# The gate's sigmoid from ScalarE's exponential and VectorE's reciprocal, with a replanned order of instructions

## The chip, the cores and the metric

The kernel runs on one core of one Trainium2 chip. The metric is the device time of one execution in microseconds (us); for the kernel before it is the median of three runs.

The engines are called by the profile's names: PE is TensorE's matrix products and PEld its weight loads, ACT is ScalarE, DVE is VectorE, POOL is GpSimd, and SP is SyncE, which issues the transfers.

## What is computed

One inference step of a two-layer decoder trunk for a prompt of 512 tokens and 64 sample tokens (8 sequences of 8), which share all weights, at model width 1024. Layer 0 mixes tokens by pooling, layer 1 by a gated DeltaNet; a SwiGLU feed-forward network of inner width 2816 follows each, and every block has a norm before and after it.

The change lies in the DeltaNet layer's gates. Cut to that, the reference is:

```python
b = proj[..., ...]; a = proj[..., ...]        # 16 value heads each
beta = jax.nn.sigmoid(b.astype(jnp.float32))
g = -jnp.exp(a_log) * jax.nn.softplus(a + dt_bias)
o, s_new = gated_delta_chunked(q, k, v, g, beta, s0)
```

`gated_delta_chunked` uses beta as a factor on keys and values, and sums of g, through exponentials, as decays.

## The kernel before

**Tiling and stages.** Activations stand with 128 channels on the partitions and 576 tokens along the free axis, split into two halves of 256 and 320 (for the feed-forward blocks 288 and 288). Each large matrix product is made of three products of split operands (`hH`, `hL` for the activations, `wh`, `wl` for the weights): ACT rounds the raw weight tile `wraw` into `wh`, DVE or POOL subtracts to give `wl`, and PE multiplies. The stages are, in order: the pooling mixer, a first feed-forward block, the DeltaNet layer in four groups of heads (loop `for G in range(GRP)`), its output projection, and a second feed-forward block.

**The start.** `tokens(tt)` (line 1235) takes a block of 128 tokens `xt`, sums its squares on ACT, takes a square root `xst`, and on DVE a reciprocal (line 1244) and the scaled tokens `xn`. The first products, against the pooling matrices `bf`, `bm` and `bh`, read `xn`. The masks `bs`, `s_in`, `s_le`, `s_st` and others are also made in that time, on POOL and DVE, for later stages.

**The gates.** `gates()` (line 1387) is called inside the first group's projection. The small tiles it uses are pieces of one buffer, `misc`. It multiplies the activations with 32 columns of the weight matrix, brings the result to token order in `ab`, takes `bet` as ACT's sigmoid of half of it, and from the other half `g`, by a softplus written as an exponential and a logarithm on ACT with DVE instructions between. The products of `g` with the triangular masks give running sums: one is copied to `gcr` by ACT and sent to the DRAM tile `gc_d`, from which decay tiles are read later. The tile `gcr` has the tag `T01`, and so does `gts` (line 1646), which the first group's sample part writes next: the later tile waits until the earlier one has been read. `bet` is scaled by the key norms later on, when the chain `rv`, `rn` on DVE has the inverse norms, and `Uw`, `BD`, `vn` read it.

**The order of the work.** All instructions from line 803 on are not issued as they are written. They are collected by the class `Plan`, with operands and dependences, and `finish` (line 431) issues them in an order that it works out when the program is built. `cost` (line 312) holds a duration for each kind of instruction. `forward` (line 568) plays the program through with one queue for each engine and picks, whenever an engine comes free, the ready instruction of best rank. `backward` turns the times of an order into due times, which are the next ranks. Where an instruction may run on DVE or POOL (`EITHER`), `forward` chooses. The transfers on SP are ordered in the same way.

ACT holds one table of functions at a time. `TABLE` (line 72) numbers the functions that need one (SiLU, exponential, square root, sigmoid, logarithm), and `TURN` gives a change of table 1283 ns in the plan. `take` (line 748) picks the next instruction of an engine; where `HOLD` is above zero for that engine, it passes over the best one if that needs another table (on PE, another mode of the array) and one that needs none is ready within `HOLD` ns of it in rank.

`forward` also keeps a picture of PE's clock: work is added up in windows of `WINDOW` ns, in four phases, since the place of the windows is not known, and a phase with less work than `LOAD` of the window has its next one at half clock. In gaps of PE over 300 ns, `idle_until` (line 614) puts in matmuls of a tile of ones into an unused bank; they are the ones written to `ps_w` from line 474.

At last, `refined` (line 480) goes over the whole order once for each string of `CHOSEN` (line 80): at each point in time it moves the ranks of coming instructions by amounts that `moved` (line 499) derives from the numbers listed there. These numbers were found by a search beforehand and stand in the source as data.

Because every planned instruction is issued from one place, nearly all lines of the profile show the same line number, 478; instructions are told apart by the tiles that they write and read.

Of the kernel before, what the change touches and what calls it, by code (L numbers as in the profile page):

```python
# [14 lines left out]
AF = mybir.ActivationFunctionType  # L15
# [27 lines left out]
VH = 16  # L43
# [14 lines left out]
class Plan:  # L58
# [15 lines left out]
    HOLD = {"PE": 2500.0, "ACT": 0.0}  # L74
    WINDOW, LOAD = 3413.0, 0.38
# [492 lines left out]
    def forward(self, rank, state=None, until=None):  # L568
# [4 lines left out]
        if state is None:  # L573
            todo = n
            left = [len(o[4]) for o in ops]
            free = dict.fromkeys(self.ENGINES, 0.0)
# [5 lines left out]
            phases = [[self.WINDOW * i / 4, 0.0, 2.0, 0, self.WINDOW * (4 - i) / 4] for i in range(4)]  # L582
            fast = 2.0
# [1601 lines left out]
```

## Time and profile before

| what | value |
|---|---|
| median of three runs | 1514.92 us (1513.43 to 1515.28) |
| the profiled execution | 1514.92 us |
| its span, from the first to the last instruction | 1513.2 us |
| mean granted clock of PE | 0.995 |
| PE busy | 1492.4 us, 99% of the span, 11790 matmuls |
| DVE busy | 1130.1 us, 75% |
| ACT busy | 852.2 us, 56% |
| POOL busy | 112.1 us, 7% |
| data moved by DMA | 197.86 MB, mean 131 GB/s |

In rows of the busy time by stage, the first figure after the stretch is its length, then comes each engine's busy time with its number of instructions, the granted clock of PE, the share of the DMA engines that was busy, and GB/s. In rows of the timeline, the first figure is the start in us from the span's start, the second the duration; a bracket at the end gives the idle time of the engine before it and what ended it. In rows of groups, behind the count stand the busy time in us, the mean of one in ns, and the idle time before. Rows of waits give the total in us, the number, and the longest. Matmuls overlap, so the interval from start to start, not the duration of one, is what a matmul takes of PE.

### The profile page before, as it was taken

Reading aid. Unit: us, or ns where it says so; the run is one execution under the profiler, and the core shown is the slowest. Engines: PE = TensorE matmul, PEld = TensorE weight load, DVE = VectorE, ACT = ScalarE, POOL = GpSimd, SP = SyncE. Lnnn points to the kernel's source line nnn. Section 1 sums busy time; section 2 is a strip of 40 time slices with the busy share of each in tenths; the row PEclk is TensorE's granted clock in tenths of the full one; section 3 lists DMA queues with packets and bytes.
Section 4 is the critical chain, followed back from the end, with each engine's and each line's share of the span. In section 5 each row is a group of like instructions: output and inputs, shape, how many; then the busy total and the mean of one; then the engine's idle time right before and its main releaser. Section 6 shows DMA issues by size and latency. Waiting matters only on the chain.

```text
span 1513.2 us, 30277 instructions
## 1 busy us (share of the span) xinstructions
PE 1492.4 (99%) x11790; PEld 1445.6 (96%) x11790; DVE 1130.1 (75%) x2280; ACT 852.2 (56%) x1839; POOL 112.1 (7%) x246
## 2 busy tenths in 40 slices
PE   8999999999999999999999999999999999999998
PEld 7999999999999899899899899899999999999997
DVE  6994566668789697996898798657796575756856
ACT  7763543435456865865684794645575453434545
POOL 4210000000001010110121110000110000000000
PEclk9999999999999999999999999999999999999999
DMA  7564233233467343434443534657864432324264
GB/s 191 146 184 127 83 88 92 80 102 111 125 181 194 90 126 111 125 99 125 130 113 94 147 113 127 199 157 215 248 193 145 127 97 86 93 81 121 65 163 136
DMA packets 344854, 197.86 MB, mean 131 GB/s; under 512 B 13499, under 2 KB 337692, under 8 KB 344703
## 3 DMA queue, kind: packets, MB, share of 16 engines
q1 hardware_dynamic: 344711, 195.92, 44.9%
q8 instruction: 93, 1.52, 0.4%
q14 instruction: 50, 0.41, 0.1%
HBM read 165.60 MB, written 30.52 MB: 130 GB/s over the span
## 4 chain that ended last, share of the span: by engine, by line
PE 57%; DVE 4%; ACT 2%; DMA 2%; issue 1%; SPq 0%; ACTq 0%; DVEq 0%
PE ps_m L478 16%; PE ps_A L478 15%; PE ps_B L478 14%; PE ps_s L478 5%; PE ps_k L478 4%; PE ps_x L478 2%; DVE vt L478 1%; DVE ac L478 1%; PE ps_n L478 1%; DMA vt<-z_d 1%; DVE wl L478 1%; DVE ii L478 0%; DMA out_dram<-St 0%; ACT wh L478 0%; DMA og<-og_d 0%
## 5 line engine op out<-in xcount | busy, mean ns | idle before, releaser
L478 ACT ACTIVATE wh<-wraw 128x1024 fp32r<-128x1024 f32 (+4 forms) x239 | 233.3, 979 | 202.6 <-PE ps_B L478 87.2
L478 DVE TENSOR_TENSOR wl<-wraw,wh 128x1024 fp32r<-128x1024 f32 (+4 forms) x238 | 266.2, 1123 | 82.8 <-ACT wh L478 48.1
L478 PE MATMUL ps_m<-hH,wh 128*128 128x320 f32 (+1 forms) x832 | 246.9, 311 | 0.3 <-ACT zz L478 0.3
L478 PE MATMUL ps_m<-hL,wh 128*128 128x320 f32 (+1 forms) x832 | 245.6, 307 | 0.0
L478 PE MATMUL ps_m<-hH,wl 128*128 128x320 f32 (+1 forms) x832 | 244.7, 307 | 0.0
L478 PEld LDWEIGHTS ps_m<-hH,wh 128*128 128x128 f32 x832 | 153.7, 189 | 4.3 <-issue 1.5
L478 PEld LDWEIGHTS ps_m<-hH,wl 128*128 128x128 f32 x832 | 154.1, 189 | 2.6 <-issue 1.3
L478 PEld LDWEIGHTS ps_m<-hL,wh 128*128 128x128 f32 x832 | 154.4, 189 | 1.9 <-issue 0.6
L478 PE MATMUL ps_B<-hH,wl 128*128 128x320 f32 (+1 forms) x444 | 128.7, 304 | 0.0
L478 PE MATMUL ps_B<-hL,wh 128*128 128x320 f32 (+1 forms) x444 | 128.4, 303 | 0.0
L478 PE MATMUL ps_B<-hH,wh 128*128 128x320 f32 (+1 forms) x444 | 128.0, 304 | 0.0
L478 PE MATMUL ps_A<-hH,wl 128*128 128x256 f32 (+1 forms) x432 | 118.9, 291 | 0.0
L478 PE MATMUL ps_A<-hH,wh 128*128 128x256 f32 (+1 forms) x432 | 118.8, 290 | 0.0
L478 PE MATMUL ps_A<-hL,wh 128*128 128x256 f32 (+1 forms) x432 | 118.4, 289 | 0.0
L478 PE MATMUL ps_A<-aL,wh 128*128 128x288 f32 (+2 forms) x408 | 113.8, 296 | 0.0
L478 PE MATMUL ps_A<-aH,wl 128*128 128x288 f32 (+2 forms) x408 | 113.4, 296 | 0.0
L478 PE MATMUL ps_A<-aH,wh 128*128 128x288 f32 (+2 forms) x408 | 113.2, 296 | 0.0
L478 PE MATMUL ps_B<-aH,wl 128*128 128x288 f32 x296 | 83.7, 297 | 0.1
L478 PE MATMUL ps_B<-aH,wh 128*128 128x288 f32 x296 | 83.0, 296 | 0.1
L478 PE MATMUL ps_B<-aL,wh 128*128 128x288 f32 x296 | 83.1, 295 | 0.0
L478 PEld LDWEIGHTS ps_B<-hH,wh 128*128 128x128 f32 x444 | 81.8, 188 | 0.3
L478 PEld LDWEIGHTS ps_B<-hH,wl 128*128 128x128 f32 x444 | 81.8, 188 | 0.1
(458 smaller groups left out, 3976.9 us busy)
## 6 DMA issues: line engine op xcount, KB each, us to landing
wraw<-in_ffn_w_in_dram SPq DMA_DIRECT2D x77, 512.0 KB
wraw<-in_gdn_w_in_dram SPq DMA_DIRECT2D x56, 512.0 KB
graw<-in_ffn_w_in_dram SPq DMA_DIRECT2D x33, 512.0 KB
wraw<-in_ffn_w_out_dram SPq DMA_DIRECT2D x32, 448.0 KB
wraw<-in_gdn_w_out_dram SPq DMA_DIRECT2D x24, 512.0 KB
wraw<-in_ffn_w_out_dram SPq DMA_DIRECT2D x32, 320.0 KB
St<-in_state_gdn_rec_dram SPq DMA_DIRECT2D x32, 256.0 KB
out_dram<-St SPq DMA_DIRECT2D x32, 256.0 KB
```

The costliest lines, as they stand in the source:

```text
L478: calls[e](*a, **k)
```

## The change

The sigmoid of the gates becomes an exponential of the negated input on ACT, an addition of 1 and a reciprocal on DVE, all in place in `bet`.

The planner is changed with it. `HOLD` for ACT goes from 0 to 1500 ns. `LOAD` goes from 0.38 to 0.40. The engines start at the times of `BEGIN`, not at zero. PE's clock is taken as full at the start (factor 1.0, before 2.0), and the first decision on it falls at `FIRST` plus a window or more. The data of `CHOSEN` are replaced: 5 strings with 2871 numbers, where there were 4 with 2377. Costs, dependences and everything else that is computed stay as they are.

```diff
     TABLE = {"Silu": 1, "Exp": 2, "Sqrt": 3, "Sigmoid": 4, "Ln": 5}
     TURN = {"PE": (130.0, 190.0), "ACT": (1283.0, 1283.0)}
-    HOLD = {"PE": 2500.0, "ACT": 0.0}
-    WINDOW, LOAD = 3413.0, 0.38
+    HOLD = {"PE": 2500.0, "ACT": 1500.0}
+    WINDOW, LOAD = 3413.0, 0.40
+    BEGIN = {"PE": 0.0, "ACT": 2250.0, "DVE": 2250.0, "POOL": 2200.0, "SP": 150.0}
+    FIRST = 4250.0
     SPARE = 1.5
...
     CHOSEN = (
-        "0: 7936 55843 86527 33991 97722 31117 8629 9687 47150 83676 16297 15132 53952 77128 31040 66847 59628 "
...
+        "0: 73658 29519 30370 59469 65203 80151 85529 43101 5733 57126 23353 4237 50459 50735 10507 95687 49324 "
...
@@ -573,14 +605,14 @@
-            free = dict.fromkeys(self.ENGINES, 0.0)
+            free = dict(self.BEGIN)
...
-            phases = [[self.WINDOW * i / 4, 0.0, 2.0, 0, self.WINDOW * (4 - i) / 4] for i in range(4)]
-            fast = 2.0
+            phases = [[0.0, 0.0, 1.0, 0, self.FIRST + self.WINDOW * (1.0 + i / 4)] for i in range(4)]
+            fast = 1.0
...
@@ -1423,7 +1455,9 @@
             ab = piece(SP1, 2 * VH)
             ACT.activation(ab, ps, AF.Copy)
-            ACT.activation(bet, ab[:, :, :VH], AF.Sigmoid)
+            ACT.activation(bet, ab[:, :, :VH], AF.Exp, scale=-1.0)
+            DVE.tensor_scalar(bet, bet, 1.0, None, op0=add)
+            DVE.reciprocal(bet, bet)
             ea = piece(VH)
             ACT.activation(ea, row[:, 0], AF.Exp)
```

322 rows, old and new, of the table CHOSEN are left out of this document.

## The prediction

> **What bounds the kernel now.** I read the head of the page first, then the busy time by stage, then who waits for whom, and last the timelines of the two places that the diff touches most plainly: the first 18 us and the gates of the DeltaNet layer.
>
> ```profile
> span 1513.2 us, 30277 instructions
> PE 1492.4 (99%) x11790; PEld 1445.6 (96%) x11790; DVE 1130.1 (75%) x2280; ACT 852.2 (56%) x1839; POOL 112.1 (7%) x246
> ...
> core 0: us, PE busy (x) PEld busy (x) DVE busy (x) ACT busy (x) POOL busy (x), PEclk, DMA share, GB/s
> 0.00:50.00 50.00, 45.25 (x300) 41.39 (x300) 34.95 (x99) 38.10 (x95) 19.80 (x79) 0.93 0.57 156
> 50.00:400.00 350.00, 349.98 (x2626) 348.47 (x2626) 247.45 (x401) 166.54 (x261) 10.47 (x10) 1.00 0.38 110
> 400.00:1050.00 650.00, 641.39 (x5441) 603.00 (x5440) 526.35 (x1251) 420.77 (x1118) 68.04 (x143) 1.00 0.49 139
> 1050.00:1500.00 450.00, 450.00 (x3396) 448.92 (x3395) 315.03 (x519) 222.23 (x357) 13.83 (x14) 1.00 0.45 132
> 1500.00:1513.20 13.20, 5.73 (x35) 3.81 (x34) 6.33 (x12) 4.52 (x12) 0.00 (x0) 0.72 0.47 151
> ```
>
> TensorE is the bound. Between 50 and 400 us and between 1050 and 1500 us it idles 0.02 us in 800 us at full clock; no order of the same matmuls wins anything there. What a new order can move lies in three places: the start (50.00 - 45.25 = 4.75 us idle, and the only granted clock below 1 ahead of the end), the DeltaNet stage (650.00 - 641.39 = 8.6 us idle) and the tail (13.20 - 5.73 = 7.5 us). Nothing in the diff touches the tail's own chain. ScalarE and VectorE have room on the whole (56% and 75%); they matter where TensorE waits for them:
>
> ```profile
> engine line waited for: us in total, times, longest us
> PE ps_x L478 <- DVE vt L478: 3.4, 5, 1.5
> PE ps_A L478 <- DVE xn L478: 2.3, 1, 2.3
> ...
> PE ps_s L478 <- DVE rv L478: 1.2, 1, 1.2
> PE ps_x L478 <- DMA crow<-in_state_gdn_conv_dram: 1.2, 1, 1.2
> PE ps_x L478 <- ACT nco L478: 1.0, 2, 0.7
> ```
>
> Two of these waits, the 2.3 us on xn and the 1.2 us laid to rv, are single events that the diff reaches.
>
> **Part 1, the planner's picture of the start.** The old planner starts all engines at 0 and holds the matrix clock to be slow (factor 2.0). The new one starts ScalarE, VectorE and GpSimd 2.2 us late and holds the clock to be full. What the chip did:
>
> ```profile
> 1.27 2.93 PE L474 MATMUL ps_w<-ones 128*128 128x128 f32 x12 [1.27 <-POOL ones L253]
> ...
> 6.04 0.28 ACT L478 ACTIVATE xst<-xst,epsd 128x1 f32<-128x1 f32 x1
> ...
> 8.47 0.38 DVE L478 COPY s_le<-s_le 64x64 f32<-64x64 f32 x1
> 8.57 0.28 DVE L478 RECIPROCAL xst<-xst 128x1 f32<-128x1 f32 x1
> 8.91 0.75 DVE L478 TENSOR_SCALAR xn<-xt,xst 128x1024 f32<-128x1024 f32 x1
> ...
> 9.71 0.49 PE L478 MATMUL ps_A<-bf,xn 128*128 128x128 f32 x2 [2.27 <-DVE xn L478]
> ```
>
> The square root that the first token block needs is done at 6.32 (6.04 + 0.28). Its reciprocal starts only at 8.57, behind mask work in VectorE's in-order queue: 2.25 us, nearly the whole 2.27 us for which TensorE then stands. A planner that lets VectorE begin at 0 expects those masks to be long over by then. One that begins it at 2.25 us sees the reciprocal ready ahead of them and will put it first. The masks (bs, s_in, s_le) have no early reader on TensorE, so they can follow at no cost. I price this at up to 2.2 us of the first idle.
>
> Right behind that gap the clock falls:
>
> ```profile
> 10.65:17.48 6.83, 6.54 (x30) 6.24 (x30) 4.72 (x12) 4.78 (x10) 3.53 (x10) 0.50 1.01 285
> 18.00:30.00 12.00, 11.45 (x97) 10.80 (x97) 7.22 (x17) 12.00 (x32) 2.36 (x1) 1.00 0.73 168
> 40.00:60.00 20.00, 20.00 (x150) 18.77 (x149) 19.73 (x57) 15.43 (x40) 6.36 (x8) 1.00 0.54 157
> ...
> 13.15 0.78 PE L474 MATMUL ps_w<-ones 128*128 128x128 f32 x2
> ...
> 16.82 0.41 PE L478 MATMUL ps_A<-dH,wl 128*128 128x256 f32 x1
> 17.03 0.41 PE L478 MATMUL ps_A<-dH,wh 128*128 128x256 f32 x1
> ...
> 21.06 0.28 PE L478 MATMUL ps_A<-dH,wh 128*128 128x256 f32 x1
> 21.18 0.28 PE L478 MATMUL ps_A<-dL,wh 128*128 128x256 f32 x1
> ```
>
> In the 6.83 us at 0.50 the 256-column matmuls follow each other every 0.21 us (16.82 to 17.03), afterwards every 0.12 (21.06 to 21.18). At full clock that stretch's work would take half, so 3.4 us are at stake if the gap ahead of it closes, or is filled with idle matmuls, and the clock holds. The bounds for the start are therefore 0 and 2.2 + 3.4 = 5.6 us. Against the whole of it speaks that ScalarE is full from 18 to 30 us (12.00 of 12.00) and VectorE from 40 to 60 (19.73 of 20.00): what TensorE gains ahead of them passes on only as far as their own work also starts earlier. It does in part, since ScalarE is busy only 4.78 of 6.83 us in the slow stretch. Neither end has the better row, so I take half, **2.8 us**.
>
> On the clock a page speaks against the new constants: the Trainium skill, TensorE: Matmul & The Clock Gate, Part 1, says that the throttled state is the default and activity releases it, so that a kernel's first matmuls run at half rate. The trace disagrees: the first twelve matmuls, at 1.27 us, take 2.93 us together, 0.24 each, where two of the same kind at 13.15, in the stretch at 0.50, take 0.39 each.
>
> **Part 2, the sigmoid.** It removes one activation with its table load and adds one exponential and two VectorE instructions.
>
> ```profile
> 523.15 0.83 PE L478 MATMUL ps_g<-t_le,misc 128*16 128x128 f32 x6
> ...
> 523.30 1.28 ACT L478 ACT_TABLE_LOAD   x1
> 524.59 0.27 ACT L478 ACTIVATE bet<-misc 128x80 f32<-128x80 f32 x1
> 524.77 0.57 ACT L478 ACTIVATE gcr<-ps_g 16x512 f32<-16x512 f32 x1
> ...
> 525.37 3.55 DMA gc_d<-gcr
> ...
> 528.94 0.42 DVE L478 TENSOR_TENSOR gts<-s_in,gHL 128x256 fp32r<-128x256 f32 x1 [1.30 <-DMA gc_d<-gcr]
> ...
> 500.00:530.00 30.00, 28.78 (x242) 24.96 (x241) 21.51 (x54) 28.07 (x79) 0.55 (x5) 1.00 0.23 65
> ```
>
> The load (1.28 us) and the sigmoid stand in ScalarE's queue ahead of the copy gcr, whose PSUM input is complete at 523.98 (523.15 + 0.83); gcr starts at 524.77. Its transfer to gc_d ends at 528.92, and only then may gts be written, because it shares gcr's buffer (tag T01); TensorE's "1.2 us on rv" is really this DMA. With the sigmoid gone from that spot, gcr can start 524.77 - 523.98 = 0.8 us earlier and the wait shrinks by the same. What is then late next is VectorE's norm chain for rv, so I take **0.8 us** and not the whole 1.2. The exponential for bet can stand beside the softplus's exponential on the same table; it needs its own load only if the order puts it elsewhere, and then this part gains 0 to 0.8 us.
>
> The additions:
>
> ```profile
> L478 DVE RECIPROCAL oss<-oss 128x20 f32<-128x20 f32 x4 | 1.1, 272 | 1.0 <-ACT oss L478 1.0
> L478 DVE RECIPROCAL nrc<-nrc 128x3 f32<-128x3 f32 x4 | 0.7, 170 | 0.4 <-ACT nrc L478 0.3
> L478 DVE SCALAR_TENSOR_TENSOR misc<-misc 128x80 f32<-128x80 f32 x3 | 0.7, 242 | 3.5 <-ACT misc L478 3.4
> ...
> L478 DVE TENSOR_TENSOR bet<-bet,rn x8: 161/164/170, 531.4 to 884.7; 128x10 f32<-128x10 f32 x8
> ...
> L478 ACT ACT_TABLE_LOAD x25 | 32.1, 1283 | 2.4 <-DMA misc<-in_gdn_a_log_dram 2.0
> ```
>
> The add of 80 elements costs about 0.24 us (the 128x80 row). No reciprocal of 80 is in the trace; from 3 to 20 elements it grows by 102 ns, 6 ns an element, which puts 80 at 272 + 60 x 6 = 0.63 us, an estimate. Together 0.87 us on VectorE, hidden: it is busy 21.51 of 30 us there and stands 3.4 us waiting for ScalarE's misc just before. Bet's first reader comes at 531.4 us. Without that cover it would cost its 0.87 us.
>
> **Part 3, ScalarE stays with its table.** HOLD for ScalarE rises from 0 to 1500: an activation that needs another table is passed over while one on the current table is less than 1.5 us behind it in rank. 25 loads take 32.1 us. Fewer loads free ScalarE, but TensorE waits for ScalarE by name hardly at all (nco, 1.0 us). At best that 1.0 us goes; at worst a passed-over activation is late for a matmul, which is a rival below. I take **0.4 us**.
>
> **Part 4, a new order everywhere.** The list of drawn seeds is replaced, five passes for four. Every engine's order changes in the DeltaNet stage; the other long stages are full whatever the order. Its bounds are its idle time, 8.6 us: all of it could go, or as much again could come. The new passes search against a start that resembles the trace, with one pass more, so I lean to a gain, but by a tenth only: **0.9 us**.
>
> **Sum.** 2.8 + 0.8 + 0.4 + 0.9 = 4.9 us off. The profiled execution took 1514.92 us (span 1513.2 and 1.7 around it), which is also the median of the three runs. 1514.9 - 4.9 = **1510.0 us**.
>
> **The rivals.**
>
> *The start's gain is absorbed* (chance 0.16). ScalarE, then VectorE, both full behind the start, keep their pace and the middle draws even: 1514.9 - 0.8 = 1514.1, within 1512 to 1517. For it: the 12.00 of 12.00. Against it: their work feeds on TensorE's and would move with it.
>
> *The held table makes TensorE wait* (0.20), the case on the slower side. A passed-over exponential or SiLU stands up to 1.5 us longer, and the transposes and products that read it wait; the profile's own waits of that kind are 0.7 us long at most (nco). If a dozen switches cost TensorE 0.7 us each, that is 8.4 us against 2.8 + 0.8 gained: 1514.9 + 8.4 - 3.6 = 1519.7. It decides from about six such waits up (4.2 us). For it: VectorE (526 of 650 us) and ScalarE (421) are fuller in that stage than in the other two long ones. Against it: the old order meets nearly all its table switches without TensorE noticing, and the limit is in rank, so urgent work still comes first.
>
> *The clock falls again* (0.06). Believing the clock full at the start, the planner puts fewer idle matmuls there; one more 6.83 us stretch at 0.50 costs 3.4 us, and with gcr's 0.8 us the time is 1517.5. The page on the clock gate would have it so; the twelve quick first matmuls speak against it.
>
> *Everything comes at its upper end* (0.10). 5.6 + 0.8 + half of the 8.6: 1504.2.
>
> That the change does not do what it says (bet's exponential with a load of its own) costs at most Part 2's 0.8 us and stays inside the forecast.
>
> **How the numbers follow.** Two tenths of a per cent, 3 us, is about what a measurement of this kernel can tell from no change; the three runs span 1.9 us. My forecast has chance 0.48, with a range of its own of 1506 to 1511.9. Faster: 0.48 + 0.10 = 0.58; same: 0.16; slower: 0.20 + 0.06 = 0.26. The range runs from 1503.0, a little below the upper-end case, to 1519.5, which leaves out half of the held-table case and the far edge of the other.
>
> **What would show it.** Right: the reciprocal of xst directly after its square root, the 2.27 us ahead of the first bf matmul below 1 us, a shorter stretch at 0.50; in the gates one load fewer and gcr straight after its matmuls, gts no longer held 1.3 us by gc_d; fewer than 25 table loads; 400 to 1050 us with 6 to 10 us of idle. Wrong: over 12 us idle in that stage with ScalarE named as releaser, or a start as long as before although its gap is closed.

## The result, and the profile after

| kernel | median | runs |
|---|---|---|
| before, on the same chip | 1514.28 us | 9 runs, 1512.40 to 1515.95 |
| after | 1516.81 us | 9 runs, 1516.27 to 1520.19 |

The ratio is 1.0026, with a 95% interval of 1.0018 to 1.0034. The change makes the kernel slower, by 0.26% over all its runs and by 2.5 us in the medians (its other runs lie further above the median than below it); the forecast was 1510.0, faster. The profiled execution took 1516.81 us. Its page, and the busy time by stage (us of the stretch, then PE, PEld, DVE, ACT, POOL, the granted clock, DMA share, GB/s):

```profile
span 1514.9 us, 30387 instructions
PE 1496.5 (99%) x11836; PEld 1448.4 (96%) x11836; DVE 1133.8 (75%) x2281; ACT 856.3 (57%) x1841; POOL 107.6 (7%) x247
...
0.00:50.00 50.00, 46.83 (x338) 42.77 (x339) 37.70 (x103) 39.06 (x96) 17.71 (x79) 1.00 0.59 168
50.00:400.00 350.00, 349.33 (x2625) 348.10 (x2625) 247.58 (x398) 164.59 (x259) 9.05 (x11) 1.00 0.38 109
400.00:1050.00 650.00, 644.34 (x5448) 604.43 (x5447) 525.71 (x1249) 425.13 (x1119) 66.97 (x146) 1.00 0.49 139
```

Read alone, these rows promise a gain: the start idles 3.2 us where it idled 4.75, its clock no longer falls, and the DeltaNet stage idles 5.7 us where it idled 8.6. The kernel is slower all the same. Part of the answer is in the rows of `ps_w`, the idle matmuls, by the same stages; first before, then after:

```profile
0.00:50.00 50.00, 4.80 (x20) 4.01 (x20) 0.93 0.57 156
...
400.00:560.00 160.00, 2.65 (x18) 2.41 (x18) 1.00 0.57 163
560.00:1050.00 490.00, 0.00 (x0) 0.00 (x0) 1.00 0.46 132
```

```profile
0.00:50.00 50.00, 9.33 (x52) 8.60 (x52) 1.00 0.59 168
...
400.00:560.00 160.00, 4.29 (x28) 3.66 (x28) 1.00 0.56 157
560.00:1050.00 490.00, 1.16 (x6) 0.94 (x6) 1.00 0.46 133
```

An idle matmul computes nothing, but it counts as busy. In the DeltaNet stage idle time and idle matmuls together are 8.6 + 2.65 = 11.3 us before and 5.7 + 4.29 + 1.16 = 11.1 us after: TensorE does without real work as long as it did, only more of it is painted over. In the start it is 4.75 + 4.80 = 9.6 us before and 3.17 + 9.33 = 12.5 us after; against these 2.9 us more stands the half-clock stretch of 6.83 us that is gone, worth up to 3.4 us.

**The start after** (start, duration, engine, what, idle before and its releaser):

```profile
1.27 5.23 PE L506 MATMUL ps_w<-ones 128*128 128x128 f32 x26 [1.27 <-POOL ones L285]
...
6.61 1.06 PE L510 MATMUL ps_A<-ident,xt 128*128 128x128 f32 x8
...
7.51 1.06 PE L506 MATMUL ps_w<-ones 128*128 128x128 f32 x8
...
7.76 0.28 ACT L510 ACTIVATE xst<-xst,epsd 128x1 f32<-128x1 f32 x1
...
8.08 0.16 DVE L510 RECIPROCAL xst<-xst 128x1 f32<-128x1 f32 x1 [1.42 <-ACT xst L510]
...
9.31 0.46 PE L510 MATMUL ps_A<-bf,xn 128*128 128x128 f32 x2
```

The reciprocal now follows the square root directly. But the planner, which takes the clock for full, has put 13 idle matmuls (26 records) where there were 6. The first transposes start at 6.61 instead of 4.42, ScalarE's copy of them stands ahead of the square root, and that ends at 8.04 instead of 6.32. Of the 2.25 us won at the reciprocal, 0.4 us are left at the first product on `bf` (9.31, before 9.71).

**The gates after**, on ScalarE, and below them the same chain before:

```profile
517.93 1.28 ACT L510 ACT_TABLE_LOAD   x1
519.22 0.27 ACT L510 ACTIVATE misc<-misc 128x80 f32<-128x80 f32 x1
519.51 1.28 ACT L510 ACT_TABLE_LOAD   x1
520.81 0.26 ACT L510 ACTIVATE qks<-ac 128x64 f32<-128x64 f32 x1
521.08 1.28 ACT L510 ACT_TABLE_LOAD   x1
522.38 0.27 ACT L510 ACTIVATE misc<-misc 128x80 f32<-128x80 f32 x1
...
524.08 1.28 ACT L510 ACT_TABLE_LOAD   x1
525.38 0.27 ACT L510 ACTIVATE bet<-misc 128x80 f32<-128x80 f32 x1
525.59 0.59 ACT L510 ACTIVATE gcr<-ps_g 16x512 f32<-16x512 f32 x1
```

```profile
519.06 0.27 ACT L478 ACTIVATE misc<-misc 128x80 f32<-128x80 f32 x1
...
519.60 1.28 ACT L478 ACT_TABLE_LOAD   x1
520.89 0.27 ACT L478 ACTIVATE misc<-misc 128x80 f32<-128x80 f32 x1
```

The exponential of `bet` has a load at its place (524.08), so nothing is saved there. (The same load also serves `gce`, an exponential at 527.30, which has none of its own here; before, it had one at 528.84.) Worse, a SiLU of 0.26 us (`qks`) is taken between the softplus's exponential and its logarithm, with a load for it: from the one to the other it takes 522.38 - 519.22 = 3.16 us, before 1.83. The limit in rank that should keep ScalarE on its table did not prevent that, and there are more loads, not fewer:

```profile
L510 ACT ACT_TABLE_LOAD x27 | 34.6, 1283 | 1.6 <-issue 1.2
```

### The profile page after: what moved, and what is told of

Read it like the earlier page. It is cut to its first block, busy times and chain, and to the rows that moved or that the text cites. A ratio compares the mean times of both kernels' runs of the same rounds, so it can differ in the third digit from the quotient of the medians.

```text
span 1514.9 us, 30387 instructions
## 1 busy us (share of the span) xinstructions
PE 1496.5 (99%) x11836; PEld 1448.4 (96%) x11836; DVE 1133.8 (75%) x2281; ACT 856.3 (57%) x1841; POOL 107.6 (7%) x247
## 4 chain that ended last, share of the span: by engine, by line
PE 88%; DVE 5%; ACT 2%; DMA 2%; issue 1%; POOL 1%; DVEq 0%; SPq 0%; POOLq 0%; ACTq 0%
PE ps_B L510 28%; PE ps_A L510 28%; PE ps_m L510 19%; PE ps_k L510 5%; PE ps_s L510 5%; PE ps_x L510 2%; PE ps_e L510 1%; PE ps_n L510 1%; DVE wl L510 1%; DMA vt<-z_d 1%; DMA wraw<-in_ffn_w_out_dram 1%; DVE y L510 1%; ACT wh L510 1%; DVE ac L510 1%; ACT L510 0%
## 5 line engine op out<-in xcount | busy, mean ns | idle before, releaser
L510 PE MATMUL ps_m<-hH,wh 128*128 128x256 f32 (+1 forms) x832 | 250.8, 312 | 1.6 <-ACT u L510 1.4
```

The costliest lines, as they stand in the source:

```text
L510: calls[e](*a, **k)
```

## The experiments

All kernels here are the program after (in a_sigmoid with the sigmoid put back), with its planner's search left out and the order of all instructions written down as a list. The list is put together from the order that the kernel before issues, called the old order, in which VectorE's two added instructions stand where the sigmoid stood, and from that of the kernel after, the new order.

```diff
-            for i, e in best[1]:
+            for i, e in listed:
```

**Which stretch of the new order loses?** Four lists. Where the gates have the old order, the exponential for `bet` stands right behind the softplus's own, on its table; where they have the new order (mid_new, and mid_new2 below), it has the load at its place, as in the kernel after.

```diff
 b_exp      old order throughout
 start_new  new order to 82 us, then old
 mid_new    old, new order from the first ps_e (453 us) to the output projection (1045 us), old
 end_new    old order to 1045 us, then new
```

> The old order, word for word, with one edit: bet comes from the exponential, placed on ScalarE right behind the softplus's first exponential, and the add and the reciprocal stand on VectorE where the sigmoid stood in the order. Theory A (the sigmoid's own table load delays gcr and so the first sample product): one load fewer (24 in place of 25 behind the first), gcr about 0.8 us earlier than 524.8, the wait of gts on gc_d 0.5 us in place of 1.3, time 0.5 to 1 us below the kernel before (1513.4). Theory B (the wait is replaced by the next one, or hidden): same loads saved, time unchanged within 0.3 us.

> The new order up to 81.5 us of its plan, the old order for all that is left; bet as in b_exp or as the old order has it. Where the traces are compared by the matrix work done, the new kernel is 1.0 us ahead at 17 us and 1.8 us ahead at 83 us. Theory A (the start is better and the loss lies later): the lead stays, time 1.5 to 2 us below the kernel before, near 1512.7. Theory B (the lead is borrowed from work of other engines that falls due behind it): time within 0.5 us of the kernel before or above it.

> The old order up to the first product of the DeltaNet projection (near 453 us) and from the output projection's second half on (near 1045 us), the new order between. The comparison by work done has the new kernel lose 1.3 us in this stretch. Theory A (the new order of the DeltaNet stage is worse by itself): 1 to 2 us above the kernel before, near 1515.8, with more than 26 table loads in all. Theory B (the stage only inherits what the stages before it leave): within 0.5 us of the kernel before.

> The old order up to the output projection's second half (near 1045 us), the new order from there. The comparison by work done has the new kernel lose 1.1 us from 1051 us to the end, 0.7 of it in the last 55 us. Theory A (the new order of the last feed-forward block and of the tail is worse): about 1 us above the kernel before, near 1515.4. Theory B (no loss of its own): within 0.4 us of it.

| kernel | median | ratio to before | 95% interval |
|---|---|---|---|
| b_exp | 1513.98 us | 0.9999 | 0.9990 to 1.0008 |
| start_new | 1514.02 us | 0.9999 | 0.9990 to 1.0008 |
| mid_new | 1518.91 us | 1.0032 | 1.0019 to 1.0044 |
| end_new | 1514.62 us | 1.0006 | 0.9997 to 1.0014 |

Of the three stretches only the DeltaNet stage shows a loss; start and end can't be told from even (by the intervals the start costs between -1.5 and 1.2 us, the end between -0.5 and 2.1). The list mid_new loses more (4.9 us against the kernel before, measured beside it) than the whole kernel after does (2.5), so part of its loss may come from putting two orders together. The exponential in place of the sigmoid is free when it stands on the softplus's table: 24 loads, and no time either way. Since b_exp computes the same as the kernel after and is even with before, what makes the kernel after slower is its order, idle matmuls and table loads included.

**Is it the idle matmuls of that stage?** mid_new2 is mid_new without the six that are there twice at the first seam; mid_new2_noidle has none at all in the new stretch.

```diff
 mid_new2_noidle
-    idle matmuls between 453 and 1045 us
```

> As mid_new, but without the twelve idle matmul records that the seam near 456 us had put in twice (13 planned ones less). Theory A (the new order of the DeltaNet stage is worse by itself): still 2 to 4 us above the kernel before, near 1517. Theory B (mid_new's loss was the seam's idle matmuls): within 0.8 us of the kernel before.

> As mid_new2, with all idle matmuls of the new stretch left out (11 planned ones, 22 records, among them 12 between 528 and 532 us). Theory A1 (part of the loss is idle matmuls that run while real work is ready): 1 us or more below mid_new2. Theory A2 (they fill time in which TensorE would stand anyway): equal to mid_new2 within 0.4 us.

Measured: 1519.79 us, ratio 1.0043 (1.0031 to 1.0055), and 1519.68 us, 1.0046 (1.0033 to 1.0059). Leaving out the idle matmuls gives nothing back. Without them the clock falls: the profile of mid_new2_noidle shows it at half from 532.0 to 535.4 us, which costs 1.7 us; whether they cost as much as that while they hold the clock, these two runs can't tell.

**Which part of the stage?** The new order in one piece of it only; in gates_new the exponential has the load of its own, as in the new order.

```diff
 proj_new   new order from 453 to 510 us
 gates_new  new order from 510 to 542 us
 rest_new   new order from 542 to 1045 us
```

> The old order, with the new one only for the first part of the DeltaNet layer (from its first convolution product, about 453 us, to about 510 us, ahead of the gates). Where the DeltaNet stage's loss of 4 to 6 us (mid_new, mid_new2) sits is asked of this run and the two beside it. Theory G (the gates' stretch, 510 to 542 us, carries most of it): this part costs 1 to 2 us, ratio 1.000 to 1.001. Theory S (the loss is spread evenly over the stage by its length, 57 of 592 us): 0.5 us, ratio 1.0003, not to be told from nothing. If this part alone costs over 3 us, both fall.

> The old order, with the new one only from about 510 to 542 us, the stretch of the gates; the exponential for bet stands there with a table load of its own and the copy gcr behind it. Theory G: 2 to 3.5 us, ratio 1.0013 to 1.0023, and a plateau of about that height in the trace from 543 us on. Theory S: 0.3 us, ratio 1.0002.

> The old order, with the new one only from about 542 us to the end of the DeltaNet layer (about 1045 us). Theory G: 0 to 1.5 us, ratio 1.000 to 1.001, though this is 85% of the stage by length. Theory S: 3.5 to 5 us, ratio 1.0023 to 1.0033.

| kernel | median | ratio to before | 95% interval |
|---|---|---|---|
| proj_new | 1518.96 us | 1.0034 | 1.0021 to 1.0047 |
| gates_new | 1516.11 us | 1.0020 | 1.0012 to 1.0029 |
| rest_new | 1516.66 us | 1.0023 | 1.0014 to 1.0032 |

Neither theory holds: each piece loses, and by their sum (some 12 us) more than the stage as a whole. The seams have a large part in that. At one seam of each list TensorE stands in a wait that neither b_exp nor the kernel after has at that place; in proj_new, gates_new and rest_new:

```profile
520.77 0.66 PE L661 MATMUL ps_x<-ident,qk 128*128 128x128 f32 x4 [1.90 <-ACT qk L661]
```

```profile
550.14 0.39 PE L661 MATMUL ps_m<-hH,wh 128*128 128x256 f32 x1 [1.22 <-ACT u L661]
```

```profile
548.25 0.44 PE L661 MATMUL ps_k<-ident,BD 128*128 128x128 f32 x2 [1.40 <-DVE ks L661]
```

The difference in time at which the same work of TensorE (without idle matmuls) is reached, against b_exp, gives their shares. For proj_new it is 0.0 us at 450 us, 1.7 us at 495 us and 4.4 us at 517 us (by the clock of b_exp's profile), so 2.7 us arise at the seam behind the piece, where the old order finds things not ready; a stretch of half clock at 714.6 us, in a piece whose order is the old one, adds 1.6 us. In gates_new 1.3 us arise in the piece and 1.5 us behind it, and in rest_new 1.6 of some 2.0 us arise right behind its seam. So the pieces do not tell which part of the stage loses. The kernel after has no seam: by the same comparison it is 1.0 us ahead of b_exp at 450 us, 2.5 us behind at 560 us and 2.0 us behind at 1055 us. That puts the loss of the stage, 3.0 us, into the projection and the gates of the first group, where the longer softplus chain stands; it rests on one profile of each.

**Is it the exchange of the sigmoid?** b_exp_place is the old order with the exponential exactly where the sigmoid stood, with a load of its own.

```diff
 b_exp_place, against the kernel before
-    ACT  bet = sigmoid
+    ACT  bet = exp
+    DVE  bet + 1, reciprocal, at once behind it in the plan
```

> The old order with the change to the sigmoid alone, the exponential where the sigmoid stood, so with a table load of its own (25 loads again, where the exponential beside the softplus's had 24). If the place of the exponential decides by itself, this is 1 to 2 us slower than that version, so ratio 1.0005 to 1.0015 against the kernel before. If only the order around it decides, it equals the kernel before: ratio 0.9995 to 1.0005; VectorE's 0.85 us for the add and the reciprocal stay hidden.

Measured: 1516.55 us, ratio 1.0023 (1.0014 to 1.0032). It is not the table load, since the sigmoid needed one there too. VectorE's timeline in b_exp_place, and then the matmul that waits for the end of that chain:

```profile
522.43 0.16 DVE L661 TENSOR_SCALAR rv<-ps_x 128x4 f32<-128x4 f32 x1 [0.53 <-PE ps_x L661]
524.06 0.20 DVE L661 TENSOR_SCALAR bet<-bet 128x80 f32<-128x80 f32 x1 [1.47 <-ACT bet L661]
524.30 0.65 DVE L661 RECIPROCAL bet<-bet 128x80 f32<-128x80 f32 x1
524.87 0.74 DVE L661 SCALAR_TENSOR_TENSOR ac<-u,cwt,ac 128x600 f32<-128x600 f32 x1
525.53 0.17 DVE L661 TENSOR_SCALAR rn<-rv 128x20 int32<-128x20 int32 x1
...
528.82 0.42 DVE L661 TENSOR_TENSOR gts<-s_in,gHL 128x256 fp32r<-128x256 f32 x1
...
529.38 0.36 PE L661 MATMUL ps_s<-gts,s_gt_r 128*128 128x256 f32 x1 [1.91 <-DVE rv L661]
```

The addition waits 1.47 us for ScalarE, which is loading a table, and in VectorE's in-order queue three convolution steps `ac`, the chain `rv`, `rn`, a weight subtraction and `gts` wait behind it, though none of them reads `bet`. They come 1.47 + 0.20 + 0.65 = 2.3 us later than they could. TensorE stands 1.91 us (b_exp: 0.35), and then the clock goes: the stretch behind that wait has half clock.

```profile
529.80:533.10 3.30, 3.30 (x15) 3.21 (x14) 1.72 (x10) 1.32 (x4) 0.95 (x1) 0.50 1.05 296
```

Half clock for 3.4 us loses 1.7 us of work; with the longer wait, 1.56 us, that is 3.3 us, which is the loss measured.

**If it is the queue, moving the two instructions must give it back.** b_exp_late leaves ScalarE as in b_exp_place and moves only these two:

```diff
 VectorE's order in b_exp_late
-    bet + 1, bet reciprocal
     ac, rn, ac, rv, ac, rv, rn, wl, rv
+    bet + 1, bet reciprocal
     gts
```

> As b_exp_place (old order, the exponential with a table load of its own where the sigmoid stood), but VectorE's add and reciprocal for bet are moved back in its queue, from ahead of three conv steps (ac), the chain rv, rn and a weight subtraction (wl) to directly ahead of gts. In b_exp_place the add stood 1.47 us waiting for ScalarE's bet with all of these queued behind it. Theory Q (that wait in the in-order queue, 1.47 + 0.20 + 0.65 us, is what made b_exp_place 3.3 us slower): back to the kernel before, ratio 0.9995 to 1.0008. Theory L (the load or the exponential itself costs it): 1.0015 to 1.003 as there.

```profile
526.43 0.17 DVE L661 SCALAR_TENSOR_TENSOR rv<-rn,rv 128x20 f32<-128x20 f32 x1
526.52 0.19 DVE L661 TENSOR_SCALAR bet<-bet 128x80 f32<-128x80 f32 x1
526.75 0.65 DVE L661 RECIPROCAL bet<-bet 128x80 f32<-128x80 f32 x1
527.32 0.36 DVE L661 TENSOR_TENSOR gts<-s_in,gHL 128x256 fp32r<-128x256 f32 x1
...
527.83 0.36 PE L661 MATMUL ps_s<-gts,s_gt_r 128*128 128x256 f32 x1 [0.56 <-DVE rv L661]
```

Measured: 1513.97 us, ratio 1.0003 (0.9994 to 1.0012). The whole loss of b_exp_place was the place of two short instructions in a queue.

**And in the new order?** There the addition waits for nothing: `bet` is ready when its turn comes. a_sigmoid takes the new order and puts the sigmoid back; a_beside takes it with the exponential moved beside the softplus's.

```diff
 a_sigmoid, against the kernel after
-    ACT bet = exp;  DVE bet + 1, reciprocal
+    ACT bet = sigmoid
```

```diff
 a_beside, against the kernel after
     ACT  misc = exp (softplus)
+    ACT  bet = exp
     ...
-    ACT  bet = exp
```

> The new order in full, but bet by ScalarE's sigmoid as in the kernel before, at the exponential's place, and without VectorE's add and reciprocal. Theory O (the new order loses by itself; the exchange of the sigmoid is free in it, since there the add waits for nothing): 1516 to 1518, ratio 1.0015 to 1.0035. Theory X (the exchange loses, the order is even): 1512 to 1514.5, ratio 0.9985 to 1.0005.

> The new order, with the one exponential of bet moved on ScalarE to right behind the softplus's first exponential. Theory A (in the new order the exponential has a table load of its own, so that the change does not do there what it says): one or two loads fewer than 27, gcr about 1.5 us earlier than 525.6, time 0.5 to 1.5 us below the new kernel. Theory B (the load is hidden there): loads fewer, time the same within 0.4 us.

Measured: a_sigmoid 1520.56 us, ratio 1.0048 (1.0030 to 1.0066); a_beside 1520.61 us, 1.0049 (1.0037 to 1.0061). Both lose far more than was expected of them, and more than the kernel after, but each edit does more than its list shows. The load ahead of `bet` in the kernel after also serves `gce`. With the sigmoid there, or with the exponential moved away, `gce` needs a load of its own: a_sigmoid has 28 loads against 27, and a_beside still has 27. This load stands where TensorE waits for it; in a_sigmoid, on ScalarE and on TensorE:

```profile
527.08 1.28 ACT L661 ACT_TABLE_LOAD   x1
...
528.78 0.43 PE L661 MATMUL ps_g<-misc,t_gt 128*128 128x64 f32 x2 [0.94 <-ACT ngs L661]
```

`ngs`, directly behind `gce`, comes 1.1 us later than in the kernel after, where this matmul does not wait; a_beside has the same wait with 0.95 us. Behind it the clock falls at the gates (in a_sigmoid again at 838.5), 3.4 us of lost work in each profile, about what the two lose against the kernel after. So they do not separate the exchange from the order; they show that one instruction exchanged or moved in this order can bring a table load, a wait and a slow stretch at another place, 3 to 4 us in all. That the order is now given as a list is not the reason: a_idle6 (below) is the new order as a list too, and its two quickest runs take 1515.79 and 1516.83 us. The kernel after stays at full clock in the same place. The rows of a_sigmoid, of a_beside, and of after:

```profile
531.30:534.60 3.30, 3.30 (x13) 2.84 (x13) 3.30 (x6) 3.26 (x7) 3.30 (x3) 0.50 0.85 247
838.50:841.80 3.30, 3.30 (x39) 3.18 (x35) 1.23 (x1) 1.50 (x4) 0.00 (x0) 0.50 0.55 152
```

```profile
531.70:538.40 6.70, 6.70 (x28) 6.18 (x27) 4.84 (x14) 4.82 (x11) 4.11 (x4) 0.50 0.95 266
```

```profile
531.30:534.60 3.30, 2.94 (x21) 2.58 (x20) 3.30 (x9) 3.27 (x10) 2.61 (x3) 1.00 1.03 319
```

**What are the thirteen idle matmuls of the start worth?** Four kernels change only their number; start_new_fill has six in the first block and seven more spread over 8 to 13 us.

```diff
 a_idle6          new order:          13 -> 6
 start_new_idle6  start_new:          13 -> 6
 start_new_idle9  start_new:          13 -> 9
 b_idle13         b_exp (old order):   6 -> 13
 start_new_fill   start_new_idle6:    + 7 between 8 and 13 us
```

> The new order, with 6 idle matmuls in place of 13 in the block ahead of the first transposes. Theory A (at the start the clock is at half although the profile shows 1.00, so that each idle matmul takes 0.43 us and not the planned 0.22, and 13 of them hold back the first transposes until 6.6 us): the first transposes at 4.4 to 4.7 us, the square root xst at 6.0 to 6.3 in place of 7.8, the first bf product before 8 us in place of 9.3, and the time 1 to 2 us below the new kernel, near 1515.3. Theory B (fewer idle matmuls leave the clock at half longer, which takes the gain back): the same earlier first transposes, then a longer stretch with records 0.21 us apart, time equal to the new kernel's or above.

> As start_new (new order to about 82 us, then the old one), with six instead of thirteen idle matmuls in the first block. The new order in full lost 5 us in four of six runs with six (a_idle6). Theory B (the missing idle matmuls let the clock fall at the start): the same here, 1517 to 1520 in most runs, ratio 1.002 to 1.004, mean clock 0.993 to 0.996. Theory D (the clock fell elsewhere, in the gates' thin stretch of the new order, which this kernel does not have): even with start_new, ratio 0.9985 to 1.0005.

> The old order with the exponential beside the softplus's (as b_exp), and thirteen idle matmuls instead of six in the first block. Theory C (thirteen idle matmuls at half rate hold the first transposes back by about 1.5 us and buy a full clock behind them): the records show no stretch at half clock between 9 and 18 us, mean clock 0.997 or more, and the time is even with b_exp, ratio 0.9985 to 1.0005, since the two cancel. Theory P (the count of idle matmuls does not set the clock there): a half-clock stretch as before and 1 to 1.5 us slower, ratio 1.0007 to 1.001.

> As start_new, with nine idle matmuls in the first block, between the thirteen of start_new (1514.0, clocks 0.996 to 0.999) and the six of start_new_idle6. If each idle matmul in the block costs its 0.21 us a record as long as the clock holds, and fewer of them only raise the share of executions with a fall of the clock: runs near 1511.5 with some near 1517, median 1511 to 1514, ratio 0.998 to 1.0005.

> As start_new_idle6, with six more idle matmuls spread over 8 to 12 us, beside the waits for xn and wh. start_new_idle6 had two kinds of execution: about 1510.3 at a mean clock of 0.998 (six of twelve) and about 1516.8 at 0.993 (five). If it is the thin stretch from 8 to 14 us that lets the clock fall, in some phases of its windows, the second kind goes or becomes rare: median 1510 to 1511.5, ratio 0.9975 to 0.999. If the clock at the start is decided by the first block of idle matmuls alone, both kinds stay and the median is 1511 to 1517 with clocks of 0.993 in about half of the runs.

| kernel | median | ratio to before (95%) | runs at a mean clock of 0.996 or more | runs at 0.993 or 0.994 |
|---|---|---|---|---|
| start_new (13) | 1514.02 us | 0.9999 (0.9990 to 1.0008) | 11: 1511.65 to 1514.97 | none |
| start_new_idle9 | 1514.42 us | 1.0008 (0.9997 to 1.0018) | 7: 1511.24 to 1515.21 | 5: 1516.70 to 1518.41 |
| start_new_idle6 | 1513.33 us | 0.9997 (0.9983 to 1.0010) | 7: 1509.81 to 1514.81 | 5: 1516.36 to 1518.39 |
| start_new_fill | 1513.09 us | 1.0002 (0.9989 to 1.0015) | 8: 1509.68 to 1513.68 | 4: 1516.86 to 1518.25 |
| a_idle6 | 1522.40 us | 1.0049 (1.0032 to 1.0066) | 3: 1515.79, 1516.83, 1522.21 | 3: 1522.59 to 1523.28 |
| b_idle13 | 1511.67 us | 0.9985 (0.9977 to 0.9994) | 11: 1510.89 to 1513.82 | none |

This is a trade. With six idle matmuls the start is quick, and the same program then has one of two times, 6 to 7 us apart, by its mean clock (0.005 less over 1514 us is 0.005 x 1514 = 7.6 us of full-clock time less). With thirteen these low mean clocks do not occur, but the first transposes come 1.7 us later (6.28 us in start_new, 4.55 in start_new_idle6). On the old order, whose start wins nothing by early transposes, the insurance alone remains, and b_idle13 is the only version whose interval lies below that of before, by 0.15%: nine of its eleven runs have a mean clock of 0.997 or 0.998, one of b_exp's eleven has. It is not a sure insurance. The profiled execution of b_idle13, its slowest (1513.82 us, mean clock 0.996), has the half-clock stretch of the kernel before, though its expectation said that there would be none:

```profile
11.20:17.90 6.70, 6.70 (x32) 6.46 (x31) 4.72 (x12) 4.34 (x10) 2.98 (x9) 0.50 0.95 249
```

The profile of start_new_idle6 is of an execution with full clock; its first product on `bf` comes 1.4 us ahead of the kernel before, at 1509.97 us in all:

```profile
1.26 2.93 PE L657 MATMUL ps_w<-ones 128*128 128x128 f32 x12 [1.26 <-POOL ones L469]
4.55 1.94 PE L661 MATMUL ps_A<-ident,xt 128*128 128x128 f32 x8 [0.36 <-POOL bm L661]
...
8.29 0.39 PE L661 MATMUL ps_A<-bf,xn 128*128 128x128 f32 x2
```

Filling the thin stretch behind the first block (start_new_fill) did not make the low clock rare: four of twelve runs. So the first block decides more than that stretch; whether another filling would do both was not tried.

## Why the prediction was wrong

**Part 4, the new order (0.9 us off): this step failed, in its sign.** b_exp, the same computation in the old order, is even with the kernel before (0.9999), and the kernel after is 0.26% above before. With the start even, the term measured is a loss of 2.5 us by the medians and 4 us by the ratios, Part 3's held table included, where gains of 0.9 and 0.4 stood. By the profiles of after and b_exp 3.0 us arise in the DeltaNet stage, none of them behind 560 us. (mid_new, mid_new2 and a_sigmoid lose 5 to 7 us, but with seams or a load that the kernel after does not have.) Which instructions of the new order do it stays open. The leaning was argued from the planner, a better picture of the start and one pass more, and not from a row. The bounds of 8.6 us on both sides held the result. The sign that the prediction set for it, 6 to 10 us of idle in that stage, came out at 5.7 and meant nothing, because the fill counts as busy.

**Part 1, the start (2.8 us off): the mechanism was right, a reading was wrong.** The reciprocal moved as foreseen, the wait on `xn` closed and the half-clock stretch went. What failed was the sentence on the first twelve matmuls. They were at half rate: twelve records in 2.93 us, the last of them 0.42 us long, give (2.93 - 0.42) / 11 = 0.23 us from start to start (0.21 but for the first step), and eight records in 1.06 us after (7.51 us) give 0.11 with the last 0.28 long. I compared durations, 0.24 against 0.39, and a granted clock of 1.00 that the page shows there only because no record of the clock comes before 7.24 us (after: 5.63 us). The Trainium skill, TensorE: Matmul & The Clock Gate, Part 1, has the throttled state as the default; the trace, read by the spacing, agrees with it. With the clock read rightly, a planner that starts at full clock is seen to underrate its idle matmuls by half, and thirteen of them, 26 records in 5.23 us, spend what the reciprocal wins: the start is even (start_new, 0.9999). The 2.8 us would not have been out of reach: the six executions of start_new_idle6 at 0.998 or more have a median near 1510.3 us, 3.1 below before; but they are picked by their clock, and the median over all twelve is even with before.

**Part 2, the sigmoid (0.8 us off): two terms failed.** The exponential got a load of its own, which the prediction allowed for, but at a cost of at most the 0.8 us. And the two VectorE instructions were called hidden by their duration; the durations were right (add 0.20 us, estimated 0.24; reciprocal 0.65 us, estimated 0.63), but the cover named, VectorE's 3.4 us of waiting for `misc`, lies ahead of `bet` and cannot cover what waits for `bet`. In the old order this costs 3.3 us (b_exp_place against before; b_exp_late gets it back); the new order happens to avoid it. The 0.8 us were also read from one slow transfer. From the issue of `gc_d` to that of its readers took 3.56 us in the profile before, 1.59 in b_exp's and 1.58 in after's, so `gts` waits for it in none of the later traces:

```profile
525.37 0.33 SPq L478 DMA_DIRECT2D gc_d<-gcr  x1
528.93 2.02 SPq L478 DMA_DIRECT2D QD<-gc_d  x4
```

```profile
526.21 0.33 SPq L510 DMA_DIRECT2D gc_d<-gcr  x1
527.79 2.02 SPq L510 DMA_DIRECT2D QD<-gc_d  x4
```

**Part 3, the held table (0.4 us off): failed.** 27 loads instead of 25, and the SiLU between exponential and logarithm makes the gates' chain 1.3 us longer. How much of the order's loss is due to `HOLD` and how much to the new lists of numbers stays open: the numbers were found for one setting of the planner, and no kernel here separates the two.

**The rivals.** The start's gain did vanish, but not because ScalarE and VectorE were full; the idle matmuls spent it. The held table as the slower case named the right stage, but its mechanism, a dozen waits for ScalarE, is not in the profile: the longest total of that kind is 1.4 us on `u`. The clock did not fall at the start. It falls at the gates, in variants of both orders, where I had not looked for it.

## What to carry to other kernels

An instruction moved to another engine costs its wait, not its duration: look at what stands behind it in the in-order queue, and put it there only when its input is sure to be ready. Count idle fill as idle when you compare two profiles, and judge the clock by the spacing of like matmuls, not by their durations or by a default. A newly planned order is a change of its own with either sign; run it with the old code, and the old order with the new code, before a loss is laid to the code. When you put a list together from two orders, or take one instruction out of an order, look first for waits and table loads that neither parent has.

## What the runs showed of the hardware

The granted clock can fall in the middle of a run, behind no gap of TensorE longer than 2.0 us: stretches of 3.4 us at half clock at 529.8 (b_exp_place), 532.0 (mid_new2_noidle), 714.6 (proj_new), 531.3 and 838.5 (a_sigmoid) and 43.4 us (start_new_idle9), and of 6.8 us at 531.6 (a_beside). At 714.6 us the order around it is the one of b_exp, whose profile has no such stretch; so it depends on more than the order there, and 2 us more or less at one place of one profile need no cause in that place's instructions. Whether a start of the same instructions is followed by a low clock changes from one execution to the next (start_new_idle6: seven and five of twelve). A table load took 1.28 us in every kernel, and an activation behind it whose input was ready began 11 or 12 ns later.
